# Three tiles of the second output projection side by side between the last heads, and the last heads' share of all four inside the next group

## The chip, the core and the metric

The kernel runs on one core of a Trainium2 chip. The metric is the device time of one execution in microseconds, lower is better. Five engines work side by side and meet through semaphores: TensorE (PE, matrix products and transposes into PSUM), VectorE (DVE), ScalarE (ACT), GpSimd (POOL) and SyncE (SP, which issues most DMAs). Each engine takes its instructions in the order in which they stand in its own queue. An instruction that waits holds back all that stand behind it.

## The reference, cut to what matters

Two layers. Layer 0 is latent attention (8 heads) and a SwiGLU network; layer 1 is attention with a bias over the relative position (16 heads of 64) and a second SwiGLU network. The change is in layer 1:

```
def chunked_mixer(h, k_band, v_band, w_q, rel_table, w_o):
    q = (h @ w_q).reshape(B, n_c, CHUNK, B_HEADS, B_HEAD_DIM)
    ...
    p = jax.nn.softmax(s, axis=-1).astype(v_band.dtype)
    o = jnp.einsum('bnhqk,bnkhd->bnqhd', p, v_band).reshape(B, S, B_HEADS * B_HEAD_DIM)
    return o @ w_o
```

and what follows it: `x + rms_norm(y, attn_post_g[1])`, then the network. There are 512 positions and 1024 features, all in float32.

## The kernel before

Every tile has 128 partitions. The features of the residual stream are 8 tiles of 128 x 512. To keep float32 precision each operand is split into a high and a low part (line 144 on ACT makes the high one, line 145 on DVE the low one), and each product is three matmuls: high by high (L356), low weights or values by high (L357) and high by low (L358). Below, three such matmuls of 128x512 that add one input tile `k` into one output tile are called a **unit**.

**Second attention.** Sixteen heads, four query tiles each, make 64 slots. In a slot stand the scores of one query tile (`sc`, L1550 and L1551), DVE's minimum with the bias (L494), ACT's exponential (L496), two slots later the transposes of the exponentials (`pt`, L508) and their split into `pth` and `ptl` (L144, L145), and once in four slots the product with the values (`pv`, L1558 and L1559). After `pv`, ACT copies half of the output (`ot`, L1564), DVE adds it to the other half (`of`, L1565). Two heads are a pair; after a pair's second `pv`, ACT spreads the sums (`rw`, L1570), PE transposes them (`rs`, L1579), DVE multiplies (`of`, L1580), and the split into `oh` and `ol` gives one of the eight tiles that the output projection takes in (`osp`).

**The filler.** Between those steps `weave` in `attention` puts units of other work from the generator `fill_b`: for each pair of heads the projections of queries and keys (16 units and a mark, `b<-xh`), and after the last pair `out_first`, the first part of the output projection (`b<-oh`). Units are handed out evenly: `rate = (units - first) / slots` a half-slot's worth at a time, here (126 - 12) / 64 = 1.78 a slot. When the last scores have been placed (`fill.scored`), up to four units follow at each of the remaining places. A head that starts calls `fill.until(pr)`, which draws its pair's projections at once if they are still missing. A unit that needs an input tile that isn't there yet yields False, and the filler stops until the next place.

**Output projection.** Its eight output tiles are made in four groups of two (`GROUPS`), each from eight input tiles and two chunks of 512 KB of weights. `out_first` makes groups 0 and 1: group 0 before, group 1 after the last scores, both without the last input tile (k = 7); those four units come at its end. `out_proj` then makes groups 2 and 3 in two halves of 256 columns, and between their steps `weave` hands the four finished tiles to `post.add` (ACT: scaled copy `y`, square `sq`; DVE: `acc`), one after every fourth step.

**What sets the order around it.** The Python order gives priorities; a scheduler then places instructions on each queue by its own idea of their times. PSUM has eight banks in three tags: `mm` four, `s` two, `t` two. Weights pass through `Feed`: five buffers `raw` for what SP loads, and three for the split chunks (`whi`, `wlo`), taken in the order of `plan_out`. SP also issues the copies that lay out queries and keys for each pair (L1533) and the loads of the biases (L1510).

The dispatch before reads:

```
while (n < 4 if fill.scored else done[0] < upto) and fill.step():
...
attention(H_B, start_b, fill, 12, 7 * 16 + 14, True)
fill.drain()
st.close()
ffn(1, a["keep"], osp, firsts)
```

Of the kernel before, what the change touches and what calls it, by code (L numbers as in the profile page):

```python
# [18 lines left out]
D, S, P = 1024, 512, 128  # L19
KT = D // P  # L20
# [3 lines left out]
H_B, HD = 16, 64  # L24
# [44 lines left out]
def trunk(ctx: ExitStack, tc: tile.TileContext, a, out):  # L69
# [22 lines left out]
    def bank(tag="mm", name="b"):  # L92
        return ps.tile([P, S], F32, tag=tag, name=name_(name), bufs={"mm": 4, "s": 2, "t": 2}[tag])
# [255 lines left out]
    feed = Feed()  # L349
# [25 lines left out]
    def run(gen):  # L375
        for _ in gen:
            pass

    def some(gen, n):
        for _ in range(n):  # L380
            next(gen, None)
# [4 lines left out]
    class Filler:  # L386
# [5 lines left out]
        def step(self):  # L392
            if self.end:
                return False
            r = next(self.gen, None)
            if r is None:
                self.end = True
            elif r is not True and r is not False:
                self.marks.add(r)
            return r is not False  # L400
# [109 lines left out]
            q_ = slice(qt * P, (qt + 1) * P)  # L510
            split(self.pt[0][:, :qt + 1, q_], self.pt[1][:, :qt + 1, q_], tv)

    def attention(n_heads, start, fill, first, units, after):


        slots = n_heads * NQT
        heads, done, late = {}, [0], []
        rate = (units - first) / slots

        def weave(upto):  # L520
            n = 0
            while (n < 4 if fill.scored else done[0] < upto) and fill.step():
                done[0] += 1
                n += 1

        for i in range(slots + 3):
            h, qt = divmod(i, NQT)
            if h < n_heads:
                if qt == 0:
                    heads[h] = start(h)  # L530
                    if h == 0:
                        weave(first)
                heads[h].scores(qt)
                fill.scored = i == slots - 1
            weave(first + rate * (i + 0.5))
            if late and not after:
                late.pop()()
            if i >= 6 and i % NQT == 2:
                t = heads.pop((i - 6) // NQT)
                late.append(t.pv(*t.pt))  # L540
            if 2 <= i < slots + 2:
                t, qt = divmod(i - 2, NQT)
                heads[t].turn(qt)
            if late and i % NQT == 3:
                late.pop()()
            weave(first + rate * (i + 1))
        if late:
            late.pop()()
# [66 lines left out]
            x.append(t)  # L615
        return x

    def out_proj(rhs, n_k, post, have, n_last):

        done = list(have)  # L620

        def weave(gen):
            for n, _ in enumerate(gen):
                if n % 4 == 3 and done:
                    post.add(done.pop(0))

        groups = GROUPS[n_k][len(have) // 2:]
        for m in groups[:-n_last]:
            b = [bank() for _ in range(m)]
            weave(proj(m, n_k, KC[m], rhs, b))  # L630
            done.extend(b)
        last = groups[-n_last:]
        ws = {}

        def half(h, i, b):
            m, n, end = last[i], 0, i + 1 == n_last
            kc = KC[m]
            chunks = range(-(-n_k // kc))
            for c in chunks[::-1] if h and end else chunks:
                size = min(kc, n_k - c * kc)  # L640
                if not h:
                    ws[i, c] = feed.next(size * m * P, not end or c + 1 < len(chunks))
                for kk in range(size):
                    n += 1
                    for j in range(m):
                        mm3(b[j][:, HALF[h]], ws[i, c]((kk * m + j) * P, P), cut(rhs[c * kc + kk], HALF[h]),
                            n == 1, n == n_k)
                        yield
                if h and end and c >= len(chunks) - 2:
                    feed.ahead(len(chunks) - 1 - c)  # L650

        b = None
        for h in range(2):
            k = KT - sum(last)
            for i, m in enumerate(last):
                before, b = b, [bank() for _ in range(m)]
                rest = half(h, i, b)
                if h and not i:
                    post.add_half(0, before, rest, 9, 8)
                elif i:  # L660
                    if not h:
                        some(rest, 2)
                    post.half(h, k - last[i - 1], before)
                weave(rest)
                k += m
        return b

# [21 lines left out]
    KC = {2: 4, 1: 8}  # L689
    GROUPS = {KT: (2, 2, 2, 2)}  # L690

    def plan_out(w, n_k):
        at = 0
        for m in GROUPS[n_k]:
            for c in range(0, n_k, KC[m]):
                feed.add(w[at][c // KC[m]], min(KC[m], n_k - c) * m * P,
                         room="h" if at == 4 and c or at == 6 else None)
            at += m

    w_o = [{2 * i: a["w_o"][l, i] for i in range(4)} for l in range(2)]  # L700

# [36 lines left out]
    plan_v(1)  # L738
    for pr in range(1, H_B // 2):
        plan_pair(pr)  # L740
    plan_out(w_o[1], KT)
    plan_ffn(1)

    x = []
# [48 lines left out]
    for j in range(2):  # L793
        t = U(name="ckv")
# [233 lines left out]
    st.close()  # L1028


    def ffn(i, x_src, osp, firsts):
        hp = tc.tile_pool(name=f"ffn{i}", bufs=1, reuse_waits="tile")
        st = ExitStack()
        hp = st.enter_context(hp)
# [6 lines left out]
        feed.room["h"] = halves_of(lambda: H(F32R, "wh"))  # L1041
        x = fetch(x_src)
        post = Post(G_APOST[i], H)
        last = out_proj(osp, KT, post, firsts, 2)
        sx = Split(x, G_FPRE[i], H)
        xs = sx.xs
        banks = [bank(), bank(), bank("s"), bank("s")]
# [465 lines left out]
    def fill_b():  # L1513
        for pr in range(H_B // 2):
            q1, k1, k2 = (pool[0].tile([P, 2, S], F32R, tag="st", name=f"{n}_{pr}", bufs=6) for n in ("q1", "k1", "k2"))
            for t in range(2):
                b = bank()
                w = feed.next(1024, False)
                for k in range(KT):
                    if k == 3:  # L1520
                        feed.ahead()
                    mm3(b, w(k * P, P), xs[k], k == 0, k == KT - 1)
                    yield True
                l = U(name="f")
                h = U(F32R, "fh")
                with first(50):
                    V.tensor_tensor(l, b, rb, op=OP.mult)
                    split(h, l, l)
                h = h.bitcast(F32)
                for e, own in enumerate((LO, HI)):  # L1530
                    for d, src, rows in (((k1, h, LO), (k1, h, HI), (k2, l, LO), (k2, l, HI)) if t else
                                         ((q1, h, LO), (q1, l, HI))):
                        nc.sync.dma_start(d[rows, e].bitcast(F32), src[own])  # L1533
            qk_b[pr] = q1, k1, k2
            yield pr
        yield from out_first(osp)

    def start_b(h):
        pr, e = divmod(h, 2)
# [47 lines left out]
        return Head(qk, lambda n: bt[:, :n][:, ::-1], lambda qt: -1.0, pv, sums[pr][:, e])  # L1587

    bias(0)
    firsts = []  # L1590
    fill = Filler(fill_b())
    for _ in range(7):
        fill.step()
# [10 lines left out]
    for tt in range(NQT):  # L1604
        v_split(b[tt], 1, tt)

    attention(H_B, start_b, fill, 12, 7 * 16 + 14, True)
    fill.drain()
    st.close()

    ffn(1, a["keep"], osp, firsts)


def _chunks(w, cols, kc):
# [85 lines left out]
```

## Time and profile before

| what | us |
|---|---|
| median of 3 runs | 1128.0 (1127.02 to 1128.33) |
| the profiled execution, device time | 1128.58 |
| its span in the profile | 1126.8 |
| DVE busy | 932.5 |
| ACT busy | 685.3 |
| PE weight loads (PEld) busy | 984.4 |

The profiled execution is 1.78 us longer than its span, and 0.58 us longer than the median. In its trace the second attention ends with the last head's `pv` at 751.78 to 753.9 us, the output projection ends at 782.2 us, and the second network follows. In a row of the timeline stand the start, the time from the first start to the last end, the engine, line, output and inputs, the shape and the count; in brackets the idle time of the engine ahead of it and what ended that. A matmul of 128x512 has a row of 0.39 us, though the next one starts 0.23 us after it, since they overlap in the array. So a stall is read here from start to start.

### The profile page before, as it was taken

How to read it: one execution, taken by the hardware profiler on the slowest of the kernel's cores; microseconds unless marked ns; L12 is line 12 of the kernel's file. 1: busy time of each engine (PE TensorE's matmuls, PEld its weight loads, DVE VectorE, ACT ScalarE, POOL GpSimd, SP SyncE). 2: the span in 40 equal slices, each digit the busy share in tenths (PEclk: the TensorE clock that was granted, in tenths of full speed). 3: DMA queues.
4: the chain of work that ended last, by engine and by line, in shares of the span. 5: the costliest groups of instructions: out<-in, count | busy, mean ns of one | idle time of the engine just before them, and what ended most of it. 6: DMA issues, size and time to landing. Idle time of an engine off the chain costs nothing.

```text
span 1126.8 us, 18993 instructions
## 1 busy us (share of the span) xinstructions
PE 1109.3 (98%) x6973; PEld 984.4 (87%) x6973; DVE 932.5 (83%) x1671; ACT 685.3 (61%) x1339; POOL 69.6 (6%) x106
## 2 busy tenths in 40 slices
PE   9999999999999999999999999999999999999997
PEld 6788889999999998887888887779999999998885
DVE  7788737999899889978857977647999899889977
ACT  6476637755555566668536777546755555566675
POOL 2200000000000002400000000000000000002402
PEclk9999999999999999999999999999999999999999
DMA  7332125323332449861456656625323322459923
GB/s 235 110 110 81 70 76 205 132 89 99 105 103 95 140 150 256 138 205 41 165 150 172 154 153 159 170 86 184 134 92 95 113 94 95 141 168 286 171 58 76
DMA packets 62990, 150.85 MB, mean 134 GB/s; under 512 B 8432, under 2 KB 10224, under 8 KB 62896
## 3 DMA queue, kind: packets, MB, share of 16 engines
q1 hardware_dynamic: 55552, 136.61, 38.6%
q0 software_dynamic: 6912, 12.59, 6.8%
q8 instruction: 55, 0.90, 0.3%
q10 hardware_dynamic: 432, 0.44, 0.1%
q14 instruction: 39, 0.32, 0.1%
HBM read 119.52 MB, written 9.63 MB: 115 GB/s over the span
## 4 chain that ended last, share of the span: by engine, by line
PE 44%; DVE 5%; ACT 2%; issue 2%; DMA 1%; POOL 0%; POOLq 0%; DVEq 0%; ACTq 0%
PE al L1434 6%; PE b L356 6%; PE b L357 6%; PE b L358 6%; PE al L1185 4%; PE be L1434 4%; PE be L1185 3%; PE ga L1434 2%; PE pt L508 2%; PE de L1185 1%; PE ga L1185 1%; DVE wlo L145 1%; DVE raw L174 1%; DMA raw<-in_w_pair 1%; PE b L1558 1%
## 5 line engine op out<-in xcount | busy, mean ns | idle before, releaser
L144 ACT CAST whi<-raw 128x1024 fp32r<-128x1024 f32 (+3 forms) x224 | 225.5, 1008 | 227.3 <-PE al L1434 74.5
L145 DVE TENSOR_TENSOR wlo<-raw,whi 128x1024 fp32r<-128x1024 f32 (+3 forms) x224 | 260.7, 1165 | 63.0 <-ACT whi L144 61.2
L1434 PE MATMUL al<-th,whi 128*128 128x256 f32 x432 | 123.4, 286 | 0.2 <-DVE ut L1446 0.2
L1434 PE MATMUL al<-th,wlo 128*128 128x256 f32 x432 | 121.4, 281 | 0.0
L1434 PE MATMUL al<-tl,whi 128*128 128x256 f32 x432 | 121.1, 280 | 0.0
L356 PE MATMUL b<-xh,whi 128*128 128x512 f32 (+1 forms) x304 | 116.8, 384 | 0.2 <-ACT xh L148 0.2
L357 PE MATMUL b<-xl,whi 128*128 128x512 f32 (+1 forms) x304 | 113.3, 373 | 0.4 <-DVE xl L149 0.3
L358 PE MATMUL b<-xh,wlo 128*128 128x512 f32 (+1 forms) x304 | 112.8, 371 | 0.0
L174 DVE TENSOR_TENSOR raw<-raw,raw 128x1024 f32<-128x1024 f32 x72 | 86.5, 1218 | 1.3 <-DMA raw<-in_w_pair 1.1
L1434 PEld LDWEIGHTS al<-th,whi 128*128 128x128 f32 x432 | 81.4, 188 | 3.1 <-DVE ut L1446 1.2
L1434 PEld LDWEIGHTS al<-th,wlo 128*128 128x128 f32 x432 | 81.4, 188 | 0.3 <-DVE wlo L145 0.3
L1434 PEld LDWEIGHTS al<-tl,whi 128*128 128x128 f32 x432 | 81.4, 188 | 0.0
L496 ACT ACTIVATE p<-p,mn 128x128 f32<-128x128 f32 (+1 forms) x96 | 54.0, 562 | 31.8 <-DVE mn L494 31.6
L145 DVE TENSOR_TENSOR ptl<-pt,pth 128x128 fp32r<-128x128 f32 (+1 forms) x96 | 46.2, 485 | 28.8 <-ACT pth L144 23.2
L144 ACT CAST whi<-wd 128x512 fp32r<-128x512 f32 x86 | 49.9, 619 | 26.8 <-PE al L1185 11.9
L145 DVE TENSOR_TENSOR wlo<-wd,whi 128x512 fp32r<-128x512 f32 x86 | 56.3, 685 | 11.5 <-ACT whi L144 11.2
L358 PEld LDWEIGHTS b<-xh,wlo 128*128 128x128 f32 x304 | 57.4, 189 | 8.8
L357 PEld LDWEIGHTS b<-xl,whi 128*128 128x128 f32 x304 | 57.5, 189 | 8.5 <-DVE xl L149 1.9
L356 PEld LDWEIGHTS b<-xh,whi 128*128 128x128 f32 x304 | 57.6, 189 | 8.3 <-ACT xh L148 1.3
L144 ACT CAST pth<-pt 128x128 fp32r<-128x128 f32 (+1 forms) x96 | 40.3, 424 | 28.5 <-PE pt L508 27.8
L1185 PE MATMUL al<-whi,ph 128*128 128x512 f32 x132 | 51.9, 393 | 0.5 <-ACT y L1246 0.5
L1185 PE MATMUL al<-whi,pl 128*128 128x512 f32 x132 | 51.5, 390 | 0.0
(309 smaller groups left out, 3264.3 us busy)
## 6 DMA issues: line engine op xcount, KB each, us to landing
raw<-in_w_pair SPq DMA_DIRECT2D x72, 512.0 KB, 3.8
wd<-in_w_down SPq DMA_DIRECT2D x54, 256.0 KB, 5.8
raw<-in_w_o SPq DMA_DIRECT2D x16, 512.0 KB, 3.6
raw<-in_w_gu SPq DMA_DIRECT2D x16, 512.0 KB, 3.6
raw<-in_w_down SPq DMA_DIRECT2D x16, 512.0 KB, 4.3
raw<-in_w_qkb SPq DMA_DIRECT2D x16, 512.0 KB, 3.6
wd<-in_w_down POOLq DMA_DIRECT2D x22, 256.0 KB, 5.8
wd<-raw POOLq DMA_DIRECT2D x22, 256.0 KB, 4.3
```

Source lines behind the costliest of these rows:

```text
L144: return (nc.scalar.copy(dst_hi, src), V.tensor_tensor(dst_lo, src, dst_hi.bitcast(F32), op=OP.subtract))
L145: V.tensor_tensor(dst_lo, src, dst_hi.bitcast(F32), op=OP.subtract))
L174: V.tensor_tensor(t, x, y, op=OP.add)
L356: nc.tensor.matmul(o, l[0], r[0], start=start, stop=False)
L357: nc.tensor.matmul(o, l[0], r[1], start=False, stop=False)
L358: nc.tensor.matmul(o, l[1], r[0], start=False, stop=stop)
L496: nc.scalar.activation(p[:, :n], p[:, :n], AF.Exp, bias=mn[:, :1], scale=-1.0, accum_out=self.sums[:, qt:qt + 1])
L508: nc.tensor.transpose(t[:, kt * P:(kt + 1) * P], p[:, kt * P:(kt + 1) * P], ident)
L1185: nc.tensor.matmul(to[e], l[c], r[d], start=j < 4 and k == 0 and n == 0, stop=k == NF // 2 - 1 and n == 2, skip_group_check=True)
L1434: nc.tensor.matmul(o, l[c], r[d], start=first_ and n == 0, stop=k == K2 - 1 and n == 2, skip_group_check=True)
L1558: nc.tensor.matmul(o[:, q_], vv, pth[:, kt, q_], start=kt == 0, stop=False)
```

## The change

The filler's last part is a new generator, `out_first_b`. Ahead of the last scores it makes **three** output tiles (0, 1 and 2) side by side, input tile by input tile, k = 0 to 6: 21 units where there were 14. Tile 3 follows after the last scores, in a bank of tag `s`, seven units where there were fourteen. The four units of k = 7 are not part of the filler any more: they are handed as `late` to `out_proj`, which runs them after six steps of its first group. That group takes its banks as one `s` and one `mm`, and then hands a finished tile to `post.add` after every second step.

`attention` is given 7 * 17 + 21 = 140 units, a rate of (140 - 12) / 64 = 2.0 a slot, and after the last scores a list of how many units may stand at each place: 0, 1, 1, 1, 1, 2, then 4. `plan_out` exchanges the second and third chunk of the weights, so that they come in the order in which three tiles side by side use them. Layer 0 keeps `out_first` and the old order (an empty `late`, four steps for each tile).

```
-    def attention(n_heads, start, fill, first, units, after):
+    def attention(n_heads, start, fill, first, units, after, pace=()):
+        pace = list(pace)
...
-            while (n < 4 if fill.scored else done[0] < upto) and fill.step():
+            most = pace.pop(0) if fill.scored and pace else 4
+            while (n < most if fill.scored else done[0] < upto) and fill.step():
...
-    def out_proj(rhs, n_k, post, have, n_last):
+    def out_proj(rhs, n_k, post, have, n_last, late):
...
-                if n % 4 == 3 and done:
+                if n % each == each - 1 and done:
                     post.add(done.pop(0))
...
-                before, b = b, [bank() for _ in range(m)]
+                first_ = late and not h and not i
+                before, b = b, [bank("s"), bank()] if first_ else [bank() for _ in range(m)]
                 rest = half(h, i, b)
+                if first_:
+                    some(rest, 6)
+                    for t in late:
+                        run(t)
...
-                weave(rest)
+                weave(rest, 2 if first_ else 4)
...
+        if in_turn:
+            chunks[1:3] = chunks[2:0:-1]
...
-        yield from out_first(osp)
+        yield from out_first_b()
+
+    def out_first_b():
+        b = [bank(name="b") for _ in range(3)]
+        firsts.extend(b)
+        ws = {}
+        def step(k, j):
+            while len(osp) <= k:
+                yield False
+            mm3(firsts[j], ws[j // 2, k // 4](k % 4 * 256 + j % 2 * P, P), osp[k], k == 0, k == KT - 1)
+            yield True
+        for k in range(KT - 1):
+            for j in range(3):
+                if k % 4 == 0 and j % 2 == 0:
+                    ws[j // 2, k // 4] = feed.next(1024, False)
+                if k % 4 == 1 and j == 0:
+                    feed.ahead()
+                yield from step(k, j)
+        while not fill.scored:
+            yield False
+        firsts.append(bank("s"))
+        for k in range(KT - 1):
+            if k == 4:
+                feed.ahead()
+            yield from step(k, 3)
+        late.extend(step(KT - 1, j) for j in range(4))
...
-    attention(H_B, start_b, fill, 12, 7 * 16 + 14, True)
+    attention(H_B, start_b, fill, 12, 7 * 17 + 21, True, (0, 1, 1, 1, 1, 2, 4))
...
-    ffn(1, a["keep"], osp, firsts)
+    ffn(1, a["keep"], osp, firsts, late)
```

How this moves PE's instructions is shown at two places. The first is PE's queue among the scores of the last head (`sc` with `q1_7`). Before, eleven rows stand there as follows; `b_..._8331` and `b_..._8332` are output tiles 0 and 1, `rs` and `pt` the transposes:

```order
L1551 MATMUL sc_1679_8431<-k2_7_8095,q1_7_8093 128x128
L357 MATMUL b_1654_8332<-ol_1620_8190,whi_1660_8354 128x512
L358 MATMUL b_1654_8332<-oh_1619_8189,wlo_1661_8355 128x512
L1550 MATMUL sc_1683_8450<-k1_7_8094,q1_7_8093 128x256
L1551 MATMUL sc_1683_8450<-k2_7_8095,q1_7_8093 128x256
L1579 MATMUL rs_1676_8418<-ident_87,rw_1668_8394 128x128 x4
L508 MATMUL pt_1682_8441<-ident_87,p_1664_8374 128x128 x3
L508 MATMUL pt_1686_8460<-ident_87,p_1673_8409 128x128 x4
L356 MATMUL b_1653_8331<-oh_1677_8424,whi_1660_8354 128x512
L356 MATMUL b_1654_8332<-oh_1677_8424,whi_1660_8354 128x512
L1558 MATMUL b_1693_8486<-pth_1669_8397,vb0_6197 128x512
```

In the changed kernel the same place of PE's queue reads as follows, where 8282, 8283 and 8284 are output tiles 0, 1 and 2, and `whi_1688` is the second chunk of weights of tile 2:

```order
L1592 MATMUL sc_1683_8456<-k2_7_8039,q1_7_8037 128x128
L356 MATMUL b_1638_8283<-oh_1568_7991,whi_1656_8335 128x512
L357 MATMUL b_1638_8283<-ol_1569_7992,whi_1656_8335 128x512
L358 MATMUL b_1638_8283<-oh_1568_7991,wlo_1657_8336 128x512
L508 MATMUL pt_1686_8466<-ident_87,p_1668_8396 128x128 x3
L356 MATMUL b_1639_8284<-oh_1568_7991,whi_1688_8474 128x512
L357 MATMUL b_1639_8284<-ol_1569_7992,whi_1688_8474 128x512
L358 MATMUL b_1639_8284<-oh_1568_7991,wlo_1689_8475 128x512
L1591 MATMUL sc_1690_8481<-k1_7_8038,q1_7_8037 128x256
L1592 MATMUL sc_1690_8481<-k2_7_8039,q1_7_8037 128x256
L356 MATMUL b_1637_8282<-oh_1625_8226,whi_1656_8335 128x512
```

Scores and transposes that followed each other directly now have a whole unit between them.

The second place is PE's queue from the last transposes to the last head's `pv` (`pth_1696`, `ptl_1697`). Before, the `pv` (8592) stands right behind them, with five matmuls of the next group (8650, in halves of 256 columns) between its first and its second:

```order
L508 MATMUL pt_1712_8585<-ident_87,p_1700_8511 128x128 x4
L1558 MATMUL b_1713_8592<-pth_1696_8499,vb0_6197 128x512
L356 MATMUL b_1727_8650<-oh_1340_7041,whi_1709_8563 128x256
L357 MATMUL b_1727_8650<-ol_1341_7042,whi_1709_8563 128x256
L358 MATMUL b_1727_8650<-oh_1340_7041,wlo_1710_8564 128x256
L356 MATMUL b_1727_8650<-oh_1397_7271,whi_1709_8563 128x256
L357 MATMUL b_1727_8650<-ol_1398_7272,whi_1709_8563 128x256
L1559 MATMUL b_1713_8592<-ptl_1697_8500,vb0_6197 128x512
```

Now fifteen matmuls of output tile 3 (8563, in a bank `s`) stand between the transposes and `pv`; twelve of them are left out here:

```order
L508 MATMUL pt_1712_8570<-ident_87,p_1707_8542 128x128 x4
L356 MATMUL b_1711_8563<-oh_1454_7519,whi_1650_8319 128x512
L357 MATMUL b_1711_8563<-ol_1455_7520,whi_1650_8319 128x512
...
L358 MATMUL b_1711_8563<-oh_1681_8449,wlo_1689_8475 128x512
L1599 MATMUL b_1713_8592<-pth_1703_8530,vb0_6197 128x512
L1600 MATMUL b_1713_8592<-ptl_1704_8531,vb0_6197 128x512
```

Behind this `pv` follow eleven matmuls of the next group (there were seven, and the five within), the transposes `rs`, seventeen more (as before) and the twelve of k = 7. In all, PE's queue holds the same 6973 matmuls of the same shapes before and after.

More of the change, by code (lines that the diff above doesn't have):

```diff
@@ L616, in fetch, with weave @@
         return x
-    def out_proj(rhs, n_k, post, have, n_last):
+    def out_proj(rhs, n_k, post, have, n_last, late):
         done = list(have)
-        def weave(gen):
+        def weave(gen, each=4):
             for n, _ in enumerate(gen):
-                if n % 4 == 3 and done:
+                if n % each == each - 1 and done:
                     post.add(done.pop(0))
@@ L690, in trunk, with plan_out @@
     GROUPS = {KT: (2, 2, 2, 2)}
-    def plan_out(w, n_k):
-        at = 0
+    def plan_out(w, n_k, in_turn=False):
+        at, chunks = 0, []
         for m in GROUPS[n_k]:
             for c in range(0, n_k, KC[m]):
-                feed.add(w[at][c // KC[m]], min(KC[m], n_k - c) * m * P,
-                         room="h" if at == 4 and c or at == 6 else None)
+                chunks.append((w[at][c // KC[m]], min(KC[m], n_k - c) * m * P, None,
+                               "h" if at == 4 and c or at == 6 else None))
             at += m
+        if in_turn:
+            chunks[1:3] = chunks[2:0:-1]
+        for chunk in chunks:
+            feed.add(*chunk)
     w_o = [{2 * i: a["w_o"][l, i] for i in range(4)} for l in range(2)]
@@ L740, in trunk @@
         plan_pair(pr)
-    plan_out(w_o[1], KT)
+    plan_out(w_o[1], KT, True)
     plan_ffn(1)
@@ L1028, in trunk, with ffn @@
     st.close()
-    def ffn(i, x_src, osp, firsts):
+    def ffn(i, x_src, osp, firsts, late=()):
         hp = tc.tile_pool(name=f"ffn{i}", bufs=1, reuse_waits="tile")
@@ L1043, in ffn @@
         post = Post(G_APOST[i], H)
-        last = out_proj(osp, KT, post, firsts, 2)
+        last = out_proj(osp, KT, post, firsts, 2, late)
         sx = Split(x, G_FPRE[i], H)
@@ L1589, in trunk @@
     bias(0)
-    firsts = []
+    firsts, late = [], []
     fill = Filler(fill_b())
```

## The prediction

> **What bounds the kernel now.** I read the page first, for the engine that is busy throughout.
>
> ```profile
> span 1126.8 us, 18993 instructions
> PE 1109.3 (98%) x6973; PEld 984.4 (87%) x6973; DVE 932.5 (83%) x1671; ACT 685.3 (61%) x1339; POOL 69.6 (6%) x106
> ```
>
> PE sets the time. Its 6973 matmuls are the same in number and shape afterwards, so the change can only remove or add time in which PE waits. All such time is 17.5 us (1126.8 - 1109.3); next I looked up, in the view by windows, how much of it lies where the change is: from the start of the second attention (about 605 us) to the second network (782 us).
>
> ```profile
> core 0: us, PE busy (x) PEld busy (x) DVE busy (x) ACT busy (x) POOL busy (x), PEclk, DMA share, GB/s
> 605.00:720.00 115.00, 114.13 (x620) 93.33 (x618) 90.91 (x219) 80.54 (x202) 1.87 (x13) 1.00 0.62 159
> ...
> 730.00:740.00 10.00, 8.97 (x47) 6.48 (x46) 7.29 (x22) 7.63 (x24) 0.00 (x0) 1.00 0.22 71
> 740.00:750.00 10.00, 10.00 (x47) 8.23 (x47) 3.99 (x8) 3.31 (x6) 0.00 (x0) 1.00 0.07 16
> 750.00:760.00 10.00, 8.91 (x58) 7.80 (x57) 3.96 (x6) 4.09 (x9) 0.00 (x0) 1.00 0.55 184
> 760.00:770.00 10.00, 9.74 (x74) 8.97 (x74) 6.38 (x10) 8.77 (x18) 0.00 (x0) 1.00 0.99 356
> 770.00:780.00 10.00, 9.37 (x80) 9.17 (x79) 7.25 (x15) 5.55 (x13) 0.69 (x1) 1.00 0.39 131
> 780.00:800.00 20.00, 20.00 (x170) 19.88 (x170) 19.93 (x54) 14.77 (x38) 0.74 (x1) 1.00 0.41 150
> ```
>
> PE is idle for 0.87 us in the first 115 us, then for 1.03, 1.09, 0.26 and 0.63 us in four of the windows of 10 us. Those four are the last heads, the end of the attention and the output projection. Between 740 and 750, where units of the output projection fill PE, it never waits. So the sum goes by these stalls one at a time, and I took them from PE's timeline. First the last heads:
>
> ```profile
> 730.01 0.39 PE L356 MATMUL b<-oh,whi 128*128 128x512 f32 x1
> 730.24 0.40 PE L357 MATMUL b<-ol,whi 128*128 128x512 f32 x1
> 730.71 0.44 PE L1550 MATMUL sc<-k,q 128*128 128x384 f32 x1
> ...
> 733.00 0.40 PE L358 MATMUL b<-oh,wlo 128*128 128x512 f32 x1
> 733.81 0.39 PE L1550 MATMUL sc<-k,q 128*128 128x256 f32 x1 [0.41 <-DVE mn L494]
> ...
> 734.74 0.49 PE L508 MATMUL pt<-ident,p 128*128 128x128 f32 x3
> 735.77 0.63 PE L508 MATMUL pt<-ident,p 128*128 128x128 f32 x4 [0.54 <-ACT pth L144]
> 736.34 0.73 PE L356 MATMUL b<-oh,whi 128*128 128x512 f32 x2
> 737.08 0.50 PE L1558 MATMUL b<-pth,vb 128*128 128x512 f32 x1
> ```
>
> Undisturbed, a 128x512 matmul starts 0.23 us after the one before (730.01 to 730.24). Against that the next start is 0.24 us late at 730.71 and 0.58 late at 733.81. Three transposes take about 0.12 each, so the four at 735.77 start 1.03 - 0.36 = 0.67 late, and 737.08 comes 0.74 - 0.46 = 0.28 after its turn. Together **1.8 us**.
>
> Idle time in the brackets is smaller (0.41 + 0.54 = 0.95 us), since a row of 0.39 us covers 0.16 us of the next one's turn. The Trainium skill (Trainium Kernel Development and Optimization, Performance Expectations) says that matmul busy time is a bad metric, because matmuls are pipelined, and that weight loads are a good one. By loads, the window from 730 us holds 6.48 us where the next holds 8.23, so (8.23 - 6.48) / 8.23 of its 10 us, 2.1 us, were lost. By idle time A to D below would come to 0.75 + 0.68 + 0.26 + 0 = 1.7 us instead of 3.3; the loads side with the starts, and so does the page.
>
> **The change part by part.**
>
> *A, the last heads.* Now a unit (three matmuls, 0.69 us) stands between nearly all neighbouring steps, as the rows of the change show. What PE has to wait for between a head's scores and their transposes is, for the widest tile:
>
> ```profile
> 733.05 0.69 DVE L494 CUSTOM_DVE_ANT_0 p<-sc,bias 128x512 f32<-128x512 f32 x1
> ```
>
> ```profile
> 733.97 0.73 ACT L496 ACTIVATE p<-p,mn 128x512 f32<-128x512 f32 x1
> ```
>
> That is 0.92 + 0.73 = 1.7 us from DVE's start to ACT's end. PE now has almost 5 us of other work between the two (fifteen matmuls of 128x512 at 0.23, nine transposes at 0.12, and four narrow ones of scores). I leave 0.2 us of waiting: **-1.6 us**. The units come from 720 to 730 us, where PE was full, so nothing is taken from a place that lacks them.
>
> *B and C, the last head's `pv` and the transposes `rs`.*
>
> ```profile
> 750.50 0.60 PE L508 MATMUL pt<-ident,p 128*128 128x128 f32 x4
> 751.78 0.51 PE L1558 MATMUL b<-pth,vb 128*128 128x512 f32 x1 [0.68 <-ACT pth L144]
> 752.12 0.28 PE L356 MATMUL b<-oh,whi 128*128 128x256 f32 x1
> 752.24 0.28 PE L357 MATMUL b<-ol,whi 128*128 128x256 f32 x1
> ...
> 754.48 0.28 PE L358 MATMUL b<-oh,wlo 128*128 128x256 f32 x1
> 755.17 0.66 PE L1579 MATMUL rs<-ident,rw 128*128 128x128 f32 x4 [0.41 <-ACT rw L1570]
> ```
>
> `pv` starts 1.28 us after the four transposes, which take 0.48: 0.80 us lost. Now fifteen matmuls (3.45 us) stand there, more than the 1.28: **-0.8 us**. A half matmul takes 0.12 us, so `rs` is 0.69 - 0.12 = 0.57 late. What it waits for is ACT's spreading of the sums:
>
> ```profile
> 753.92 0.59 ACT L1564 COPY ot<-b 64x512 f32<-64x512 f32 x1 [2.19 <-PE b L1559]
> 754.41 0.71 ACT L1570 COPY rw<-sums 128x256 f32<-128x256 f32 x2
> ```
>
> ```profile
> 754.54 0.68 DVE L1565 TENSOR_TENSOR of<-b,ot 64x512 f32<-64x512 f32 x1 [2.09 <-ACT ot L1564]
> ```
>
> Eleven halves stand between where seven stood, 4 x 0.12 = 0.48 more, though the copy can't come sooner: about 0.15 us stays, **-0.4 us**. From `rs` to the four k = 7 units stand seventeen halves as before, so their wait for `oh` and `ol` stays as it is; behind it in PE's queue all the rest of the projection would wait.
>
> *D, the finished tiles.* From 759 to 768 us ACT handles four finished tiles and the weights of the last two groups, and PE waits for split weights:
>
> ```profile
> 764.61 0.28 PE L357 MATMUL b<-ol,wh 128*128 128x256 f32 x1
> 764.97 0.50 PE L358 MATMUL b<-oh,wh 128*128 128x256 f32 x2
> ...
> 765.90 0.28 PE L358 MATMUL b<-oh,wh 128*128 128x256 f32 x1
> 766.27 0.38 PE L356 MATMUL b<-oh,wh 128*128 128x256 f32 x1
> ...
> 771.58 0.28 PE L358 MATMUL b<-oh,wlo 128*128 128x256 f32 x1
> 772.49 0.44 PE L435 MATMUL tot<-ident,acc 128*128 128x128 f32 x2 [0.63 <-DVE acc L426]
> ```
>
> The two are 0.24 and 0.25 late. In the new order ACT's queue splits these weights after one finished tile instead of two, about 1.2 us sooner: **-0.5 us**, bounded by 0 and, by the window's lower PE and load shares, about -1.
>
> *E, the sums.* At 772.49 `tot` is 0.79 late behind DVE's `acc`. Four more matmuls (0.5 us) now stand ahead of it, but DVE's queue then has a weight split between the two steps that follow, and nineteen matmuls instead of thirty cover those. I put **0**, between -0.8 and +0.8.
>
> *Earlier heads.* 2.0 units a slot instead of 1.78 make the pairs even. PE idles 0.87 us there; I put **0**, between -0.9 and +1.
>
> *Weights and banks.* The exchanged chunks cost the same two loads. Of four `mm` banks three are now held from head 13 (of 0 to 15) to the end, so the last `pv`'s bank must be empty when the next group's second tile starts, eleven halves and `rs` after it: 1.3 + 0.5 = 1.8 us. By the rows of `ot` and `of` it is empty at 755.22, some 1.5 us after `pv`'s last start. It fits by 0.3 us: **0**.
>
> The Trainium skill (PSUM — Partial Sum Buffer, Summary: rules for kernel authors) says to evacuate promptly, as PSUM is tight, which speaks against holding three banks over three heads. If one wide operation of 0.7 us came ahead of `of`, the stall would be 0.4 us and the sum -2.9 instead of -3.3; no wait of this kind is in the trace of before, where the tiles held two.
>
> Sum: -1.6 - 0.8 - 0.4 - 0.5 = **-3.3 us**. The profiled execution took 1128.58 us (span 1126.8 and 1.78 around it), so it would become 1125.3. Its median stands 0.58 lower, at 1128.0, and the forecast goes by that: **1124.7 us**, -0.29%.
>
> **The rivals.**
>
> *Weights late.* The split weights have three buffers, and three tiles side by side keep two chunks at once, so tile 2's second chunk can be split only when the first chunk's last product is done, and the next group's first chunk only when tile 3 has passed k = 3.
>
> ```profile
> 746.02 1.05 ACT L144 CAST whi<-raw 128x1024 fp32r<-128x1024 f32 x1 [2.87 <-PE b L357]
> ```
>
> ```profile
> 747.11 1.23 DVE L145 TENSOR_TENSOR wlo<-raw,whi 128x1024 fp32r<-128x1024 f32 x1 [3.50 <-ACT whi L144]
> ```
>
> A split takes 2.3 us (746.02 to 748.34). PE has 3.7 us of other work at the first place (rows between tile 1's k = 3 and tile 2's k = 4) and 4.1 at the second. Were ACT and DVE each a wide operation or two behind, about 1 us would be lost at each: -1.3 in all, 1126.7 us. For it: DVE was busy for 79% of 605 to 720. Against it: 1.4 to 1.8 us of slack.
>
> *Given back.* From 780 us DVE is busy 19.93 of 20 us beside a full PE. If DVE's work there can't start sooner, PE waits for it by what it gained: 1128.0 us. Against it: that work begins with products that follow the `tot` transposes, so it moves with PE, and DVE has 2.75 us idle between 770 and 780.
>
> *More than it says.* With the earlier heads' 0.87, E's 0.8 and the rest of A, C and D: -5.4, 1122.6 us.
>
> *Slower: the copies for the last pair.* Queries and keys are laid out by copies that SP issues in order.
>
> ```profile
> SPq L1533 <- ACT pth L144: 19.1, 5, 6.0
> ```
>
> One wait of SP here lasted 6.0 us. The last pair's first scores now come 6.9 us of PE's work after its last projection (33 rows of PE's queue); the copies must be issued and land within that. If SP is held for 6.0 us at this place, and eight copies and their landing take as long as they did, PE stands still for up to 6 us: -3.3 + 6 = +2.7, 1130.7 us. It turns slower than before (by over 0.2%) from a wait of 5.6 us on. Against it: the pair's projections are now even with the slots and not drawn at the last moment, and in the trace of before no such wait stands on PE.
>
> **How the numbers follow.** Forecast 55% (1123.5 to 1125.9), weights late 17%, more than it says 13%, given back 10%, slower 5%. The range reaches from just below the better case's time to the middle between "weights late" and "given back": **1122.4 to 1127.4**. A measurement tells about 0.2%, here 2.3 us, from no change. Faster by more than that (below 1125.7): all but a little of the forecast and the better case, **0.66**; same **0.29**; slower **0.05**.
>
> **What would show each step.** A: in PE's timeline, among the scores of heads 14 and 15 no start more than 0.2 us late, and weight loads near 8.2 of 10 us. B: no wait at the last `pv`. C: `rs` at most 0.2 late. D: no 0.24 us gaps in the next group's `b<-oh,wh` rows. E: the sum of the waits at `tot` and at the transposes `bc` that follow. If the idle time of PE from 605 to 720 grows by over 1 us, or a wait stands at tile 2's k = 4 or at the last pair's first scores, the forecast is wrong.

## The result and the profile after

Before took 1127.68 us (median; 1127.02 to 1128.33), the changed kernel **1121.64 us** (1120.31 to 1123.01). The ratio is 0.9946, with a 95% interval of 0.9934 to 0.9957. That is 6.0 us less where 3.3 were forecast, and 0.8 us below the low end of the range. Its profiled execution took 1122.24 us, 6.34 less than that of before. One execution of a later run (the tiles alone) took 1812.46 us at a granted clock of 0.56 and is in none of the ratios below.

First the page of the changed kernel: the span, and the engines' busy time.

```profile
span 1120.5 us, 18982 instructions
PE 1104.6 (99%) x6973; PEld 984.4 (88%) x6973; DVE 932.4 (83%) x1671; ACT 685.5 (61%) x1339; POOL 69.1 (6%) x106
```

The matmuls are the same 6973, yet PE's busy time fell by 4.7 us (1109.3 to 1104.6) and its idle time by only 1.6 (17.5 to 15.9), while the span fell by 6.3. Most of what was won had been booked as *busy*: a row of 0.39 us covers part of the next one's late start.

The view by windows, with the columns as before:

```profile
core 0: us, PE busy (x) PEld busy (x) DVE busy (x) ACT busy (x) POOL busy (x), PEclk, DMA share, GB/s
605.00:720.00 115.00, 114.14 (x625) 95.32 (x624) 93.36 (x221) 81.77 (x202) 1.89 (x13) 1.00 0.62 164
720.00:730.00 10.00, 10.00 (x58) 8.63 (x57) 4.79 (x17) 5.99 (x17) 0.00 (x0) 1.00 0.56 142
730.00:740.00 10.00, 10.00 (x57) 8.33 (x56) 6.84 (x17) 6.57 (x17) 0.00 (x0) 1.00 0.17 54
740.00:750.00 10.00, 10.00 (x58) 8.53 (x57) 4.61 (x10) 4.75 (x10) 0.00 (x0) 1.00 0.16 47
750.00:760.00 10.00, 10.00 (x74) 9.37 (x74) 6.40 (x9) 7.62 (x15) 0.00 (x0) 1.00 0.93 310
760.00:770.00 10.00, 9.24 (x79) 9.04 (x77) 6.28 (x11) 5.82 (x14) 0.20 (x1) 1.00 0.73 276
```

From 605 to 720 us PE's idle time is what it was (0.86 us, before 0.87), but the weight loads rose from 93.33 to 95.32 us: the same 115 us hold 2% more work. Busy time says that nothing happened there, and loads say that some 2 us did. The Trainium skill (Trainium Kernel Development and Optimization, Performance Expectations) calls loads the better metric, and these rows agree. The loads give the direction and not the size: by starts, as worked out below, PE lost 3.4 us in this window before and 2.1 after, so 1.3 us were won in it.

What still waits is in the view of waits, PE alone, from 600 us to the end:

```profile
PE tot L435 <- DVE acc L426: 0.8, 1, 0.8
PE rs L1620 <- DVE ptl L145: 0.7, 3, 0.2
PE bc L469 <- POOL r L452: 0.3, 1, 0.3
PE al L1446 <- DVE ut L1458: 0.3, 1, 0.3
```

The waits at `sc`, `pt` and the last head's `pv` are gone. Those at `tot` and `bc` are the ones that the forecast put at nothing.

**Where it came from.** For each trace I added up what PE's rows take undisturbed (start to start 0.2285 us for a matmul of 512 columns, 0.175 for 384, 0.117 for 256, 0.060 for 128, 0.108 for a transpose and 0.085 behind a run of them) and subtracted that from each row's start. How far this lag grows over the same amount of work is what a stage loses. Stage limits are given in the times of before. (Slightly below 0 means a little faster than these constants.)

```
stage of before, us       600-728  728-748  748-758  758-768  768-790    sum
its work                  earlier  last     last pv, next     sums
                          heads    heads    rs       group    tot, bc
lag gained, before          3.38     2.47     1.64     1.17     0.96    9.62
lag gained, after           1.93    -0.12     0.39     0.02     1.46    3.68
difference                 -1.45    -2.59    -1.25    -1.16    +0.50   -5.95
forecast (step)            0        -1.6 A   -1.2 B,C -0.5 D   0 E     -3.3
```

The sum explains the time: 5.95 us of the 6.34 between the two profiled executions. Only B and C have the size that was forecast.

In PE's timeline after the change, among the scores of the last heads:

```profile
734.06 0.39 PE L358 MATMUL b<-oh,wlo 128*128 128x512 f32 x1
734.29 0.28 PE L1591 MATMUL sc<-k,q 128*128 128x256 f32 x1
734.40 0.28 PE L1592 MATMUL sc<-k,q 128*128 128x256 f32 x1
734.52 0.39 PE L356 MATMUL b<-oh,whi 128*128 128x512 f32 x1
734.75 0.39 PE L357 MATMUL b<-ol,whi 128*128 128x512 f32 x1
734.98 0.40 PE L358 MATMUL b<-oh,wlo 128*128 128x512 f32 x1
735.21 0.60 PE L508 MATMUL pt<-ident,p 128*128 128x128 f32 x4
735.57 0.47 PE L356 MATMUL b<-oh,whi 128*128 128x512 f32 x1
```

Scores, unit and transposes each start 0.23 us behind the matmul of 512 columns ahead of them, and no row waits. The last head's product and the transposes behind it:

```profile
746.89 0.39 PE L358 MATMUL b<-oh,wlo 128*128 128x512 f32 x1
747.12 0.40 PE L1599 MATMUL b<-pth,vb 128*128 128x512 f32 x1
...
749.59 0.28 PE L357 MATMUL b<-ol,whi 128*128 128x256 f32 x1
749.81 0.66 PE L1620 MATMUL rs<-ident,rw 128*128 128x128 f32 x4
750.22 0.36 PE L356 MATMUL b<-oh,whi 128*128 128x256 f32 x1
```

`pv` follows at once; `rs` comes 0.22 us after a row that takes 0.12, so 0.1 late.

### The profile page after: what moved, and what is told of

Read it like the earlier page. It is cut to its first block, busy times and chain, and to the rows that moved or that the text cites. A ratio compares the mean times of both kernels' runs of the same rounds, so it can differ in the third digit from the quotient of the medians.

```text
span 1120.5 us, 18982 instructions
## 1 busy us (share of the span) xinstructions
PE 1104.6 (99%) x6973; PEld 984.4 (88%) x6973; DVE 932.4 (83%) x1671; ACT 685.5 (61%) x1339; POOL 69.1 (6%) x106
## 4 chain that ended last, share of the span: by engine, by line
PE 46%; DVE 3%; DMA 2%; issue 1%; ACT 1%; POOL 0%; SPq 0%; POOLq 0%; DVEq 0%; ACTq 0%
PE al L1446 8%; PE b L356 6%; PE b L357 6%; PE b L358 6%; PE be L1446 4%; PE al L1197 4%; PE be L1197 3%; PE ga L1446 2%; PE pt L508 1%; PE de L1197 1%; PE ga L1197 1%; PE b L1600 1%; PE b L1599 1%; PE sc L1592 1%; PE sc L1591 1%
```

## The experiments

The change has three parts that can stand alone: the **rate** of units (140 instead of 126), the **pace** after the last scores, and the **tiles** (three side by side, with the exchanged chunks). I ran them in other combinations, then the rest of what was open. The table gives the differences to before by stage, as above, and the medians; before's stands beside each, from the same chip.

```
                      600-728 -748  -758  -768  -790    sum   median  before   ratio [95%]
rate, pace, tiles      -1.45 -2.59 -1.25 -1.16 +0.50  -5.95  1121.64 1127.68  0.9946 [.9934 .9957]
  the same again       -1.37 -2.59 -1.26 -1.06 +1.49  -4.79  1122.42 1127.69  0.9953 [.9941 .9966]
rate                   -1.49 -1.18 -0.04  0.00 +0.85  -1.86  1124.54 1126.94  0.9976 [.9966 .9986]
pace                   +0.03 -0.05 -1.31 -1.12 -0.59  -3.04  1122.78 1127.05  0.9964 [.9951 .9976]
tiles                  +0.07 -1.78 -0.02 -0.80 +0.42  -2.11  1124.73 1127.05  0.9977 [.9968 .9986]
rate, pace             -1.48 -1.16 -1.32 -1.14 -0.27  -5.37  1122.37 1127.69  0.9955 [.9941 .9968]
pace, tiles            +0.06 -1.65 -1.42 -1.15 +0.02  -4.13  1121.40 1126.94  0.9951 [.9939 .9963]
rate, tiles            -1.31 -2.44  0.00 -0.82 +0.73  -3.84  1121.68 1126.94  0.9950 [.9938 .9962]
all, each 4            -1.37 -2.61 -1.37 -1.14 -0.25  -6.75  1119.51 1126.94  0.9937 [.9925 .9949]
all, each 4, rs later  -1.98 -2.63 -1.37 -1.14 -0.24  -7.36  1120.15 1127.69  0.9934 [.9922 .9947]
before, each 2         +0.05 -0.01 -0.02 +1.44 -0.08  +1.37  1128.11 1127.69  1.0007 [.9998 1.0015]
all, tot and bc later  -1.42 -2.59 -1.25 -1.13 +0.99  -5.40  1131.53 1127.48  1.0033 [1.0018 1.0048]
  with each 4, rs too  -2.23 -2.62 -1.37 -1.14 +0.16  -7.21  1129.36 1127.48  1.0013 [1.0002 1.0025]
```

The first four columns repeat within 0.25 us wherever the same code runs there. The medians tell the rate alone and the tiles alone from the whole change, but no pair of parts from it (an interval is some 2.5 us wide): by them, taking out any one of the three costs nothing that shows. They differ from the sums by up to 1.5 us, since the rest of the kernel scatters: at 600 us, ahead of every change but the last two rows', the traces stand between 2.9 us ahead of before's and level with it. (The last two rows lose theirs outside these stages.) So parts are read from the stages, one trace for each kernel.

**The same kernel again.**

> The changed kernel again, to see how far one execution's stages repeat: by stage within 0.2 us of the first time from the second attention on to 790 us (-5.95 against before), while the first 600 us and the second network differ by up to 2 us from execution to execution of any kernel. If instead the stages differ by 0.5 us or more, no stage's price below that can be told.

Four stages came within 0.1 us, the sums' stage 1.0 us apart. So that stage is no property of the order alone; see E below.

**The rate taken out of the changed kernel.**

```
-    attention(H_B, start_b, fill, 12, 7 * 17 + 21, True, (0, 1, 1, 1, 1, 2, 4))
+    attention(H_B, start_b, fill, 12, 7 * 16 + 14, True, (0, 1, 1, 1, 1, 2, 4))
```

> The changed kernel with the old rate of units (126 instead of 140, so 1.78 a slot instead of 2.0), three tiles and all else kept. Theory 'evenness': the gain that the forecast lacked comes from the rate, which no longer draws units in bursts at a pair's end and leaves the slots after them bare; then the 1.2 us gained before 728 us go, and most of the 2.5 us among the last heads (their slots are bare again), 3.0 to 3.8 us of 6.04: 1124.6 to 1125.4 us. Rival 'three tiles': the gain belongs to the tiles side by side and what follows them; then only the 1.2 us of the earlier heads go: 1122.8 us. Rival 'scatter': the 1.2 us before 728 us are one execution's scatter: up to 720 us its profile stands where that of after stands, and the time is 1121.6.

"Scatter" fell: the 1.5 us of the earlier heads are gone, to 0.1 us of before. Of the last heads' 2.6 us 0.9 went, not most of it. The time doesn't show it: 1121.40 us is next to the number of "scatter" (1121.6), 1.4 us better than the stages' sum. This trace stood 2.9 us ahead of before's at 600 us, ahead of any change.

**The rate alone, in the kernel before.**

```
-    attention(H_B, start_b, fill, 12, 7 * 16 + 14, True)
+    attention(H_B, start_b, fill, 12, 7 * 17 + 21, True)
```

> The kernel before with nothing changed but the rate of units (140 instead of 126). Theory 'evenness': -1.2 us before 728 us and -1.6 to -2.0 among the last heads but the two bare slots at the end, with the end of the attention and the projection as before: 1124.5 to 1125.2 us. Rival 'three tiles': units run out earlier, and what is gained before 728 us is lost in the last slots, where now four slots' worth less stands: 1127 to 1128 us.

"Evenness" holds, at 1124.54 us: -1.49 in the earlier heads, as with all parts, and -1.18 in the last, less than forecast, as its units run out two slots before the end. What the even rate does can be counted in PE's rows: matmuls of units between one group of a head's scores and the next. Before, the units still missing when the next pair was needed came in bursts of 19, 23 and 20 (from 660, 678 and 699 us), and behind the first of them the next three groups had 0, 2 and 0. (A run of 24 from 720 us is the output projection's.) With 2.0 units a slot the largest run is 11, the others are 7 or fewer. One wait in a bare slot, in PE's timeline in the trace of before, behind the second burst:

```profile
692.96 0.40 PE L357 MATMUL b<-xl,whi 128*128 128x512 f32 x1
693.20 0.40 PE L358 MATMUL b<-xh,wlo 128*128 128x512 f32 x1
693.78 0.66 PE L1579 MATMUL rs<-ident,rw 128*128 128x128 f32 x4 [0.19 <-ACT rw L1570]
```

`rs` starts 0.58 us after a row that takes 0.23, so 0.35 late, of which only 0.19 is idle time. But the waits at `rs` are not what the even rate takes away: four starts of `rs` in this stage are over 0.12 us late, 1.34 us together before and 1.52 with the rate alone. What goes are late starts of the transposes `pt`, from six (1.28 us) to one (0.36). All starts over 0.12 us late fell from 2.75 to 2.24 us, and the rest of the 1.49 lies in many smaller ones, which no run separates.

**The pace taken out.**

```
-    attention(H_B, start_b, fill, 12, 7 * 17 + 21, True, (0, 1, 1, 1, 1, 2, 4))
+    attention(H_B, start_b, fill, 12, 7 * 17 + 21, True)
```

> The changed kernel without the pace after the last scores: units are drawn four at a time again, and between the last transposes and the last product with the values stand six halves (0.7 us) instead of eleven halves' and fifteen whole matmuls' room. Theory: the wait of B returns, 0.5 to 0.8 us: 1122.1 to 1122.4 us, and a wait on pth stands at the last head's product. Rival: the same products stand elsewhere and cover other waits as well: 1121.6 us, no such wait.

All 1.25 us of B and C came back, more than expected, and at another place: with `pv` only 0.1 late, as the rival said, it is the transposes that wait. Of D 0.3 us came back too.

```profile
748.34 0.27 PE L1600 MATMUL b<-ptl,vb 128*128 128x128 f32 x1
749.89 0.66 PE L1620 MATMUL rs<-ident,rw 128*128 128x128 f32 x4 [1.11 <-ACT rw L1611]
```

The time (1121.68 us) is the rival's number, within a scatter that is wider than the price; the stage tells.

**The pace alone; rate and pace; the tiles alone.** The first two are the kernel before with those arguments in the call (and the lines of `weave` that read the pace), the third is the changed kernel without either.

```
 pace alone:      attention(H_B, start_b, fill, 12, 7 * 16 + 14, True, (0, 1, 1, 1, 1, 2, 4))
 rate and pace:   attention(H_B, start_b, fill, 12, 7 * 17 + 21, True, (0, 1, 1, 1, 1, 2, 4))
 tiles alone:     attention(H_B, start_b, fill, 12, 7 * 16 + 14, True)
```

> The kernel before with the pace after the last scores alone: two tiles at a time, the old rate. Theory 'the pace holds whole products back': nothing before 741 us (0 +- 0.1), -1.3 at the last head's product and its transposes, and another -1.15 at the next group's products, whose halves are then used later while ACT splits their weights at the same place of its queue: -2.4 us by 768 us, the sums' wait -0.3 to +0.9 behind it, 1125.0 to 1126.0 us beside 1127.5. Rival 'three tiles make D': without them the gaps of 0.25 us in the next group stay: -1.3 us by 768 us.

> The kernel before with the even rate (140) and the pace after the last scores, but still two tiles at a time. By stage, read at equal work of PE against the kernel before. Theory 'parts add up': -1.3 to -1.5 us before 728 us and -1.2 among the last heads, as the even rate alone gave, -1.3 at the last head's product and its transposes, as the pace alone took away from the changed kernel, and nothing at 758 to 771 us; the sums' wait between -0.5 and +0.9: about -3.5 us in all, 1123.4 us beside 1126.9. Rival: with two tiles the units are used up when the pace begins, so the pace has nothing to hold back and the time stays where the even rate alone put it: 1124.5 us.

> The changed kernel with the old rate and without the pace: what the three tiles side by side (with their exchanged chunks and the last head's part in the next group) are worth alone. Theory: nothing before 728 us, -1.7 us among the last heads, as with the old rate and the pace, nothing at the last head's product and transposes (the halves stand there again): -1.7 us by 758 us, at most -0.9 in the next group, the sums' wait up to +0.9: 1125.5 to 1126.5 us beside 1127.5. Rival: the three tiles need the rate or the pace to have units left for the last heads; alone they give nothing, 1127.0 us or more.

The pace alone gives B and C in full (-1.31) and D too (-1.12) with two tiles; "three tiles make D" fell. (Its time, 1122.78 us, is 2.2 below the forecast; its trace stood 1.8 ahead at 600 us.) Rate and pace together took 1122.37 us where the changed kernel took 1122.42 beside it on the same chip. It lost nothing of B, C and D; against "parts add up" D came on top, so 5.4 us instead of 3.5. The tiles alone gave -1.78 among the last heads, as expected, -0.80 in the next group, and 1124.73 us. There, rate and tiles help at the same place: -1.18 and -1.78 apart, -2.44 to -2.61 together.

**The finished tiles' pace.** In the changed kernel one tile after four units instead of two, the rest at the group's end; and the other way round in before.

```
-                weave(rest, 2 if first_ else 4)
+                weave(rest, 4)
+                while first_ and done:
+                    post.add(done.pop(0))
```

> The changed kernel with the finished tiles handled one after four units of the next group, not after two (the last two of them at the group's end, in a row), as before the change. Theory of D: the next group's weights then wait behind two finished tiles again, 0.5 to 1.15 us lost, in gaps of 0.24 us at its last products: 1122.1 to 1122.8 us. Rival: D's gain comes from the three tiles being finished at all by then, and the order of the rest costs nothing: 1121.6 us.

```
-                if n % 4 == 3 and done:
+                if n % each == each - 1 and done:        (each = 2 in the second network)
```

> The kernel before with nothing changed but the finished tiles of the second projection, handled after two units each instead of four. Theory 'queue of weights': the three splits that stand between the third and the fourth tile now stand behind the fourth, about 1.3 us of ACT later; the gaps of 0.24 to 0.25 us at the next group's products grow by up to 1 us together: 1127 to 1128 us where before is 1126.9. Rival: the splits have slack in that order, and the gaps come from the loads; then nothing changes there, and the sums, which stand earlier in the queues, come sooner: 1126.2 to 1126.9 us.

In the first, D kept its 1.14 us and the sums' stage gained 0.75 (1119.51 us), so the theory of D fell: the forecast's reason (splits after one tile, not two) isn't needed. But the order does matter there: in before, three splits put behind two more tiles cost 1.44 us in that stage, as its view of waits on PE names it:

```profile
PE b L356 <- ACT wh L144: 1.4, 1, 1.4
```

Its time, 1128.11, has 1 within its interval.

**The transposes `rs` half a slot later**, on top of that.

```
-            if late and not after:
+            if late and (not after or i % NQT == 0):
                 late.pop()()
...
-            if late and i % NQT == 3:
+            if late and i % NQT == 3 and not after:
```

> The changed kernel with the finished tiles one after four units, and with the transposes that spread a pair's sums half a slot later, behind the next slot's scores and unit. Theory: the 0.24 to 0.50 us that these transposes start late at most pairs' ends before 728 us go, about 1.5 us by start to start, without a new wait: 1118.0 us beside 1119.5 for the finished tiles alone. Rival: what follows them (the pair's normalised product, and through it the units of the projection and the last tiles) comes too late by as much, or the late start moves to the next transposes: 1119.5 us.

It gained 0.6 us by stage, not 1.5. The wait view has no `rs` any more, but the next transposes start up to 0.5 us late instead. With 1120.15 us it stands 2.3 below the changed kernel on the same chip (1118.94 to 1121.36 against 1121.18 to 1123.37), the best version by stages; from the one without the later `rs` no time tells it.

**The sums' steps further apart**, on the changed kernel and on the best version.

```
-                    post.add_half(0, before, rest, 9, 8)
+                    r0 = post.add_half(0, before, rest, 12, 0, True)   (without the transposes bc)
...
                     post.half(h, k - last[i - 1], before)
+                    if h:
+                        some(rest, 5)
+                        post.r[0] = spread(r0, 0)
```

> The changed kernel with the two steps of the sums further apart from what they wait for, in both networks: tot after twelve units of the half instead of nine, and the transposes bc five units into the next half instead of after eight more in the same. Theory: the waits at tot (0.92 and 1.92 us in two executions) and bc (0.48 and 0.50) come from a weight split that stands ahead of the squares in ACT's queue and itself waits for its transfer; three more units (1.07 us) ahead of tot and no wait at bc leave 0 to 0.9 us of it: 1.2 to 1.6 us less than the changed kernel, 1120.4 to 1120.8 us on the chip where that took 1122. Rival: the second network's first products wait for the normalised x by as much as bc comes later; then the wait reappears behind 772 us, and the time stays.

> The same step on top of the kernel with the finished tiles one after four units and the later transposes of the sums. There tot stood only 0.21 us late and bc not at all, since its split stands behind the squares. Theory: at most 0.2 us gained here (and what the first network's same step gives): 1119.5 to 1120.1 us on the chip where before took 1127.7. Rival as for the other run: later bc, later normalised x, 0.5 us or more lost behind 772 us.

Neither came: 1131.53 and 1129.36 us. Up to 790 us the sums' stage is about where it was without this step (+0.99 beside +0.50 and +1.49; on the best version +0.16 beside -0.24), and the wait at `tot` didn't go (1.6 us in this execution). What was lost stands later, and in the first network too. In PE's timeline of the first of the two runs, in the second network:

```profile
812.61 0.39 PE L358 MATMUL b<-xh,wlo 128*128 128x512 f32 x1
815.53 0.65 PE L469 MATMUL bc<-ident,r 128*128 128x128 f32 x4 [2.53 <-POOL r L452]
```

That is 2.7 us late at one place, and about the same in the first network. It isn't the rival's late x: the power that POOL takes for this norm (`r`) starts 2.5 us behind the transposes `tot`, where it starts 3.7 us behind them in the changed kernel. But it takes 5.40 us instead of 1.46. POOL's timeline in the changed kernel, then in this run:

```profile
805.49 1.46 POOL L452 TENSOR_TENSOR r<-v,mhalf 128x4 f32<-128x4 f32 x1 [25.01 <-DVE eps L1091]
```

```profile
810.08 5.40 POOL L452 TENSOR_TENSOR r<-v,mhalf 128x4 f32<-128x4 f32 x1 [24.13 <-DVE eps L1096]
```

At 1.46 us it would have ended at 811.54, ahead of the turn of `bc` at 812.84. It took 5.40 us in both networks of both runs and 1.45 to 1.46 at these two places in all the other traces. Each of the four times it ended 0.86 to 0.87 us after DVE's queue next fell idle; whether it waited for DVE no run tests, so the cause stays open.

Two more losses follow in these traces. The networks' products `al` waited 3.8 us for DVE's `ut` (1.3 in the second run, 0.3 in the changed kernel). And the granted clock fell to a half for 3.4 us, once in the first run's trace (from 278.4 us, at the end of a wait of 2.4 us) and twice in the second's (from 226.7 and 813.8 us, each within 3 us of a wait at `bc`). Matmuls of 512 columns then start 0.43 us apart instead of 0.23, some 1.7 us lost each time. PE's timeline of the second run, in the first network:

```profile
227.17 0.63 PE L358 MATMUL b<-xh,wlo 128*128 128x512 f32 x1
227.59 0.63 PE L356 MATMUL b<-xh,whi 128*128 128x512 f32 x1
```

The changed kernel's trace has a clock below full only in its last 4.4 us.

## Why the prediction was right and wrong

- **Earlier heads: 0 forecast, -1.45 measured.** This is the step that failed: without this gain the time would have been about 1123.1 us, inside the range. It took PE's idle time (0.87 us) as all that could be had there, though the prediction itself had shown that idle time counts about half of a stall. By starts the stage lost 3.38 us. The change that gives it was named (even pairs) and priced at nothing; the rate alone, in the kernel before, gives all of it (-1.49), and without the rate it is gone (+0.06). Through which waits it does so is shown only in part (the late `pt` above). Two smaller misses add to it: A and D were sized 1.0 and 0.7 us too small.
- **A, -1.6 forecast, -2.59 measured.** Mechanism right, size too small: the four stalls read add up to 1.8, but the stage lost 2.47 from 728 to 748 us. What was left out are smaller late starts, above all that of the row *behind* a stall: behind 733.81, for one, the head's second scores start 0.22 us later where 0.12 is usual. The 0.2 us kept in hand weren't needed either. Nearly half of A doesn't need the three tiles: the rate alone gives -1.18.
- **B and C, -1.2 forecast, -1.25 measured**, and the pace alone gives it (-1.31).
- **D, -0.5 forecast, -1.16 measured.** A third gap wasn't read, and each gap makes the next start 0.1 late. PE's timeline of before, behind the rows shown there:

```profile
766.50 0.28 PE L357 MATMUL b<-ol,wh 128*128 128x256 f32 x1
766.61 0.28 PE L356 MATMUL b<-oh,wh 128*128 128x256 f32 x1
766.73 0.28 PE L357 MATMUL b<-ol,wh 128*128 128x256 f32 x1
767.09 0.39 PE L358 MATMUL b<-oh,wh 128*128 128x256 f32 x1
```

  767.09 is 0.25 us late; and 766.50 stands 0.23 after 766.27 where 0.12 is usual. As to the reason: the pace alone, with ACT's queue at the tiles as before, gave the same 1.1 us, and so did one tile after four units. Tiles without the pace gave -0.80 to -0.82, the rate alone nothing. So several orders remove these gaps, each without the others; which of them did it in the changed kernel wasn't separated further.
- **E, 0 forecast, +0.50 and +1.49 measured.** The bounds of 0.8 either way were too narrow on the bad side. In the changed kernel PE waits at both steps:

```profile
766.51 0.28 PE L357 MATMUL b<-ol,wh 128*128 128x256 f32 x1
767.54 0.44 PE L435 MATMUL tot<-ident,acc 128*128 128x128 f32 x2 [0.76 <-DVE acc L426]
...
769.96 0.28 PE L358 MATMUL b<-oh,wh 128*128 128x256 f32 x1
770.55 0.43 PE L469 MATMUL bc<-ident,r 128*128 128x128 f32 x2 [0.31 <-POOL r L452]
```

  The forecast looked at DVE's queue; the cause begins ahead of it in ACT's. ACT's timeline in the first execution, then in the second of the same program:

```profile
764.32 1.05 ACT L144 CAST whi<-raw 128x1024 fp32r<-128x1024 f32 x1 [1.84 <-DMA raw<-in_w_gu]
765.27 0.65 ACT L425 ACTIVATE sq<-b 128x256 f32<-128x256 f32 x2
```

```profile
765.23 1.05 ACT L144 CAST whi<-raw 128x1024 fp32r<-128x1024 f32 x1 [2.93 <-DMA raw<-in_w_gu]
766.19 0.65 ACT L425 ACTIVATE sq<-b 128x256 f32<-128x256 f32 x2
```

  A split of the second network's weights stands ahead of the squares, and waits for its transfer; the transfer came 0.9 us later in the second, and `tot` with it. DVE's half of the same split stands ahead of `acc` and ends last. DVE's timeline in the first execution:

```profile
765.40 1.23 DVE L145 TENSOR_TENSOR wlo<-raw,whi 128x1024 fp32r<-128x1024 f32 x1 [2.44 <-ACT whi L144]
766.54 0.95 DVE L426 TENSOR_TENSOR acc<-acc,sq 128x256 f32<-128x256 f32 x2
```

  With the finished tiles one after four units squares and `acc` stand ahead of both halves of the split, and `tot` is only 0.2 us late. ACT's timeline there:

```profile
762.34 0.74 ACT L425 ACTIVATE sq<-b 128x256 f32<-128x256 f32 x2 [1.24 <-PE b L358]
762.98 0.83 ACT L565 ACTIVATE y<-b,gains 128x256 f32<-128x256 f32 x2
764.53 1.05 ACT L144 CAST whi<-raw 128x1024 fp32r<-128x1024 f32 x1 [0.72 <-DMA raw<-in_w_gu]
```

- **The rivals.** No wait at tile 2's second chunk, at the next group's first, or at the last pair's first scores: weights and SP's copies were in time, and the banks too. Nothing was given back in the second network (-0.4 us more by the end). What came is nearest to "more than it says", which got 13% and put the earlier heads at 0.87. Its own terms (0.87, 0.8, and 0.2, 0.15 and 0.5 for the rest of A, C and D) add up to -5.8 and 1122.2 us, not -5.4 and 1122.6, so that the range's low end cut it off. The chances of faster came out on the right side.
- **What the change owes to its name.** With two tiles, rate and pace gave the same time within the scatter (1122.37 against 1122.42 us). By stages the three tiles add 1.4 us among the last heads, and E takes 0.8 to 1.8 of it back, which goes with the finished tiles' pace and not with the three tiles (E is -0.25 with one after four units). That the last head's part is called after six steps of the next group moves no instruction: PE, ACT and DVE have the same order if these steps are called at its start, so nothing is ascribed to it.

## What to carry to other kernels

Where an engine is full, price a stage by its lag at equal work (starts against undisturbed starts, summed over the whole stage), not by idle time and not by the few largest gaps: here idle time showed 0.87 of 3.4 us. Look at numbers that spread filler (a rate, a pace) before the structure around them; two arguments of one call gave, within the scatter, the time of the whole change. And in a queue, put what waits for a transfer behind what the busy engine waits for, and after any reordering compare the durations of the same operations, not only their order: what a later step of the sums cost here came from one operation on POOL that took 5.40 us instead of 1.46.

## What was not expected

A stall costs more than its gap: at three places of before, in two stages, the start behind a late one was late by another 0.10 to 0.11 us (733.81, 764.97, 766.27). One and the same program differs by 1.0 us in one stage, through a transfer's arrival, while four other stages repeat to 0.1 us. And the later sums cost little up to 790 us, but with them POOL's `r` took 5.40 us instead of 1.46 in both networks, and the runs scattered more (1126.77 to 1135.44 us). That scatter goes with the mean granted clock: the shortest of these ten executions had 0.998, the longest 0.993.
